# Narrow products in a position table, a second bank for two blocks' transposes, and VectorE rows for the last routed tile

## The chip, the cores and the metric

The program runs on one core of one Trainium2 chip. The metric is the device time of one execution in microseconds (us). The kernel before was timed three times: 1193.30, 1194.58 and 1198.49 us; the median, 1194.58 us, is its time.

## The reference, cut to what matters

One layer of a decoder trunk on 1024 tokens of width 1024, in fp32: a mixing half (attention beside a convolution), a residual sum, a second RMS norm, and a mixture of 32 experts (top 1 of 4 groups, then the top 2 of that group's 8 experts), another residual sum and a last norm. The change lies where the mixing half ends and the experts begin:

```
x = x + gt1 * mix
h2 = rms_norm(x, g_norm2[l]) * (1.0 + sc2) + sh2          # rows the experts read
# hier_moe, per token:
grp = argmax(h2 @ w_rg + b_rg)                              # 1 of 4 groups
top_val, top_idx = top_k(expert logits of that group, 2)    # 2 of its 8 experts
top_w = softmax(top_val) * p_grp
# per expert, on its tokens only:
y = (silu(xb @ w_gate[e]) * (xb @ w_up[e])) @ w_down[e]
x = x + gt2 * (sum over the token's two experts of top_w * y)
out = rms_norm(x, g_final)
```

## The kernel before, in words

**The stages.** The first half of the time is the mixing half. Then, tile by tile (`tt` 0 to 7, 128 tokens each), the output projection adds the residual (`second_norm`), makes the normed rows `h2`, stores them to DRAM (`h2d`), and routes the tile (`route`). The expert stage follows: expert after expert, a gather of the expert's rows from `h2d`, transposes, the gate and up products, a transpose of the hidden rows, the down products, and a scatter-add.

**Routing a tile.** `second_norm` sums the squares on ScalarE, forms the reciprocal root `r` on GpSimd (`rstd_of`, L93 and L94), transposes the raw rows to `xT` and returns `logits`, which multiplies by the router weights (L804) and scales by `r` (L806). The rows `h2 = x*r*a2b + sh2b` are made by two VectorE instructions (L794, L795) for tiles 0 to 6; for tile 7 GpSimd multiplies, ScalarE scales by `r` and GpSimd adds (L790 to L792). `route` is a chain of small VectorE instructions (L715 to L754), two products for the rank of each token in its expert, and two products (L760) that scatter token numbers and weights into the table `ptab` (4 values, 2 rounds of slots, 32 experts), summed over all tiles in one bank. After tile 7 the columns of the first four experts (`LO` = 4) are copied out (L881) and turned into the gather indices `early_t` (`tables`), the whole table is copied to `tb` (L883), and the first gathers may start.

**Position tables.** Experts from number 4 on are reordered at run time by how many tokens they have, so that some can be packed in half tiles (`PK`). `position_tables` does this in small steps between the products of the first two experts: it transposes the table (L1148), counts, ranks, and brings the columns into the new order with four groups of small products, the first two for packed experts in halves of 64 columns (L1202), the last two whole with 128 columns (L1205). From `pos`, which comes out of it, the queue of loads takes the number of every expert from 4 on.

**The expert stage.** Weights come through a ring of 8 buffers of 2 MB, filled by the sync queue (L595) in the order of use; a buffer is loaded again when its last reader is done. An expert that isn't packed has its weights split into a high and a low part, in four pieces per matrix, ScalarE making the high part (`ehi`, L102) and VectorE the low one (`elo`, L105); each product is done three times (high by high, high by low, low by high; L1028 to L1030). In this stage TensorE, VectorE and ScalarE run in the order in which the code is written. The rows of an expert are transposed in two steps of four 128x128 blocks (`x_steps`, L997), each into the tile `pt` of the pool `psx`, which has one buffer; ScalarE and VectorE then make `xh` and `xl` out of it. The pool `psg` has two buffers each for `pg` and `pu`, the sums of gate and up.

Ahead of the expert stage a scheduler orders the instructions of each engine.

Of the kernel before, what the change touches and what calls it, by code (L numbers as in the profile page):

```python
# [43 lines left out]
def trunk_kernel(ctx, tc, x, c, w_mod, b_mod, g_norm1, w_in, conv_w, conv_b, conv_ln_g, conv_ln_b,  # L44
# [663 lines left out]

    def route(tt, lg):
# [43 lines left out]
        for q in range(2):  # L753
            v.scalar_tensor_tensor(s0[:, :, :, q], rk[:, ks, None].to_broadcast([P, 2, 4]), float(P), Sf[:, ks, :],  # L754
                                   op0=OP.is_ge if q else OP.is_lt, op1=OP.mult)
        RH = wk3.tile([P, 2, 8, E], F32R, name="RH", bufs=1)
        v.tensor_tensor(RH, OH[:, ks, None, :].to_broadcast([P, 2, 8, E]),
                        s0.rearrange("p k a q -> p k (a q)")[:, :, :, None].to_broadcast([P, 2, 8, E]), op=OP.mult)
        for k in range(2):
            nc.tensor.matmul(ptab, onehots(8 * k + tt), RH[:, k, :, :], start=(tt == 0 and k == 0),  # L760
                             stop=(tt == 7 and k == 1), skip_group_check=True)
# [10 lines left out]
    def second_norm(tt, po):  # L772
# [8 lines left out]
        r = rstd_of(wk3, ss, 1, 1.0 / D)  # L781
        xT = mhp.tile([P, 8, P], F32, name="xT", tag=f"qk{2 + tt % 2}")
# [5 lines left out]
        if tt == 7:  # L788

            gp(h2, xt, a2b, OP.mult)  # L790
            nc.scalar.mul(h2, h2, r)
            gp(h2, h2, sh2b, OP.add)  # L792
        else:
            v.scalar_tensor_tensor(h2, xt, r, a2b, op0=OP.mult, op1=OP.mult)  # L794
            v.tensor_add(h2, h2, sh2b)  # L795
# [40 lines left out]
    for tt in range(2, 8):  # L836
# [3 lines left out]
        if tt % 4 == 3:  # L840
# [13 lines left out]

    early_t, late_t = [[rtc.tile([P, n], dt, name=f"{nm}{n}") for nm, dt in (("ti", I32), ("ws", F32))]
                       for n in (LO, E - LO + 1 + NOV)]

    half_t = [rtc.tile([P, E - LO + 1], dt, name=f"{nm}h") for nm, dt in (("ti", I32), ("ws", F32))]
    tb = rtc.tile([P, 4, 2, E], F32, name="tb")

    def slots(e):

        if e < LO:
            return [t[:, e:e + 1] for t in early_t]
        return [t[:, e - LO:e - LO + 1] for t in (half_t if e in PK else late_t)]

    def tables(tb, dst, pool, halves=False):

        ti, ws = dst
        n = tb.shape[-1]  # L870
        em = pool.tile([P, n], F32, name=f"em{n}", bufs=1)
        v.tensor_scalar(em, tb[:, 0, :], 0.0, BIG, op0=OP.is_equal, op1=OP.mult)
        if halves:
            v.scalar_tensor_tensor(em, tb[:, 0, :], -1.0, em, op0=OP.add, op1=OP.add)
            v.tensor_scalar(ti, em, 2.0, upper, op0=OP.mult, op1=OP.add)
        else:
            v.scalar_tensor_tensor(ti, tb[:, 0, :], -1.0, em, op0=OP.add, op1=OP.add)
        v.tensor_add(ws, tb[:, 2, :], tb[:, 3, :])

    t0 = wk3.tile([P, 4, LO], F32, name="t0", bufs=1)  # L880
    v.tensor_copy(t0, ptab[:, :, 0, 0:LO])  # L881
    tables(t0, early_t, wk3)
# [89 lines left out]
    def x_steps(e):  # L972
# [21 lines left out]
        def step(kk):  # L994
            pt = psx.tile([P, 4, P], F32, name="pt")
            for k in range(4):
                nc.tensor.transpose(pt[:, k, :], xt[:, 4 * kk + k:D:8], ident)  # L997
            split(xh[:, 4 * kk:4 * kk + 4, :], xl[:, 4 * kk:4 * kk + 4, :], pt)
# [138 lines left out]
    def position_tables():  # L1137
# [59 lines left out]
        for q, c0, c1, halves in jobs:  # L1197
            w = c1 - c0
            for a in range(4):
                sl = slice(o + a * w, o + a * w + w)  # L1200
                for h in range(2) if halves else ():
                    nc.tensor.matmul(c[64 * h:64 * h + 64, sl], tT[:, q, a, 0:64], pi[:, c0:c1], start=True, stop=True,  # L1202
                                     skip_group_check=True)
                if not halves:
                    nc.tensor.matmul(c[:, sl], tT[:, q, a, :], pi[:, c0:c1], start=True, stop=True, skip_group_check=True)  # L1205
# [233 lines left out]
```

## Time and profile before

| what | value |
|---|---|
| times | 1193.30, 1194.58, 1198.49 us |
| the profiled execution's own time | 1195.03 us |
| its span, first to last instruction | 1193.2 us |
| TensorE busy | 1079.5 us (90%) |
| VectorE busy | 784.2 us (66%) |
| ScalarE busy | 514.3 us (43%) |
| GpSimd busy | 232.0 us (19%) |
| DMA, mean over the span | 245 GB/s |
| mean granted TensorE clock | 0.957 of full speed |

The span is 1.8 us shorter than the execution's time; what lies around it is not touched here. In the rows below, PE is TensorE's products, PEld its weight loads, DVE is VectorE, ACT ScalarE, POOL GpSimd, and SPq the queue from which SyncE issues transfers. PEclk is the granted clock of TensorE: 1.00 is 2.4 GHz and 0.50 is 1.2 GHz. A product's busy time is longer than the distance to the next product, since products overlap; distances are read from the starts.

### The profile page before, as it was taken

The page shows a single profiled execution, that of the slowest core. Times are in us where ns is not written, and L with a number is a line of the kernel's source. Part 1 is how long each engine was busy: PE and PEld are TensorE (multiplying, and loading weights), DVE is VectorE, ACT ScalarE, POOL GpSimd, SP SyncE. Part 2 cuts the span into 40 slices and gives each one's busy share as a digit, 9 for nine tenths or more (in the row PEclk, how much of TensorE's full clock was granted, in tenths as well). Part 3 has the DMA queues.
Part 4 walks back from the last instruction along what each step waited for, and adds up shares of the span by engine and source line. Part 5 has one row for each costly group of instructions (what it writes and reads, how often), then busy time and mean ns, then how long its engine had stood idle before and what let it go on. Part 6 is the DMA issues. An engine that isn't in the chain of part 4 may idle for free. (4 is left out here: it accounts for less than half of the span.)

```text
span 1193.2 us, 16040 instructions
## 1 busy us (share of the span) xinstructions
PE 1079.5 (90%) x5876; PEld 788.5 (66%) x5876; DVE 784.2 (66%) x1300; ACT 514.3 (43%) x801; POOL 232.0 (19%) x204
## 2 busy tenths in 40 slices
PE   3899999999899999999789999999979998898960
PEld 0667777777566666888667877777656676576740
DVE  1457999992765656767658866666654586485833
ACT  2431112112767664322346655555553474364613
POOL 2340000003312104100211322222211131231112
PEclk9799999999799999999879999999999999999995
DMA  9542624302011005834757999999999999999947
GB/s 365 203 150 81 247 106 165 117 1 88 1 36 36 1 1 204 319 142 177 299 196 258 352 396 408 407 401 378 394 390 383 391 383 374 381 399 373 392 127 288
DMA packets 60829, 292.65 MB, mean 245 GB/s; under 512 B 11862, under 2 KB 16214, under 8 KB 33093
## 3 DMA queue, kind: packets, MB, share of 16 engines
q1 hardware_dynamic: 48020, 253.16, 54.2%
q0 software_dynamic: 11296, 34.17, 10.0%
q10 hardware_dynamic: 1424, 4.20, 0.9%
q8 instruction: 48, 0.79, 0.3%
q14 instruction: 41, 0.33, 0.1%
HBM read 275.75 MB, written 26.23 MB: 253 GB/s over the span
## 5 line engine op out<-in xcount | busy, mean ns | idle before, releaser
L105 DVE TENSOR_TENSOR elo<-raw,ehi 128x1024 fp32r<-128x1024 f32 x228 | 270.6, 1219 | 95.0 <-ACT ehi L102 93.4
L102 ACT CAST ehi<-raw 128x1024 fp32r<-128x1024 f32 x228 | 234.1, 1049 | 101.5 <-DMA raw<-in_w_exp_down_dram 36.7
L317 DVE SCALAR_TENSOR_TENSOR cv<-cv,cwT 128x1024 f32<-128x1024 f32 x120 | 154.1, 1284 | 3.6
L269 PE MATMUL pb<-hT,whi 128*128 128x512 f32 x256 | 100.8, 394 | 1.7 <-POOL hT L98 1.3
L268 PE MATMUL pb<-hT,whi 128*128 128x512 f32 x256 | 101.7, 399 | 0.0
L270 PE MATMUL pb<-hT,wlo 128*128 128x512 f32 x256 | 100.3, 392 | 0.6 <-DVE wlo L105 0.6
L1104 PE MATMUL py<-ehi,hh 128*128 128x512 f32 x152 | 63.4, 417 | 8.2 <-ACT ehi L102 6.7
L1073 POOL DMA_INDIRECT x1d<-ys,ti x19 | 44.9, 2361 | 129.2 <-DVE ys L1117 114.3
L1105 PE MATMUL py<-elo,hh 128*128 128x512 f32 x152 | 61.7, 406 | 4.4 <-DVE elo L105 4.4
L1028 PE MATMUL pg<-ehi,xh 128*128 128x512 f32 x152 | 62.5, 412 | 0.0
L268 PEld LDWEIGHTS pb<-hT,whi 128*128 128x128 f32 x256 | 48.1, 188 | 21.8 <-ACT whi L102 9.2
L1106 PE MATMUL py<-ehi,hl 128*128 128x512 f32 x152 | 60.6, 399 | 0.9 <-DVE hl L105 0.9
L1029 PE MATMUL pu<-elo,xh 128*128 128x512 f32 x152 | 60.1, 395 | 0.7 <-DVE elo L105 0.7
L1029 PE MATMUL pg<-elo,xh 128*128 128x512 f32 x152 | 60.5, 398 | 0.0
L1030 PE MATMUL pg<-ehi,xl 128*128 128x512 f32 x152 | 60.5, 398 | 0.0
L1028 PE MATMUL pu<-ehi,xh 128*128 128x512 f32 x152 | 59.9, 394 | 0.0
L1030 PE MATMUL pu<-ehi,xl 128*128 128x512 f32 x152 | 59.8, 393 | 0.0
L269 PEld LDWEIGHTS pb<-hT,whi 128*128 128x128 f32 x256 | 48.1, 188 | 13.0 <-POOL hT L98 2.9
L916 POOL DMA_INDIRECT xe<-h2d,ti x20 | 28.6, 1430 | 138.8 <-PE pt L997 122.9
L1017 PE MATMUL pu<-raw,x 128*64 128x256 f32 x448 | 51.6, 381 | 4.2 <-DMA raw<-in_w_exp_up_dram 4.2
L270 PEld LDWEIGHTS pb<-hT,wlo 128*128 128x128 f32 x256 | 48.1, 188 | 10.7 <-DVE wlo L105 1.0
L422 ACT ACTIVATE ns<-ns,st 128x128 f32<-128x128 f32 (+7 forms) x64 | 49.2, 772 | 9.2 <-DVE st L418 8.6
(276 smaller groups left out, 2203.5 us busy)
## 6 DMA issues: line engine op xcount, KB each, us to landing
raw<-in_w_exp_gate_dram SPq DMA_DIRECT2D x64, 1024.0 KB
raw<-in_w_exp_up_dram SPq DMA_DIRECT2D x64, 1024.0 KB
raw<-in_w_exp_down_dram SPq DMA_DIRECT2D x64, 1024.0 KB
wm<-in_w_mod_dram POOLq DMA_DIRECT2D x16, 1024.0 KB, 5.1
wm<-in_w_mod_dram SPq DMA_DIRECT2D x8, 1024.0 KB
raw<-in_w_in_dram SPq DMA_DIRECT2D x3, 2048.0 KB
xt<-in_x_dram SPq DMA_DIRECT2D x8, 512.0 KB
raw<-in_w_in_dram SPq DMA_DIRECT2D x4, 1024.0 KB
```

Of the source, the lines that this page charges most:

```text
L102: nc.scalar.copy(hi, src)
L105: nc.vector.tensor_sub(lo, src, hi.bitcast(F32))
L268: nc.tensor.matmul(p[half], hi[:, k, :], hT[0][:, k, sl], start=(k == 0), stop=False)
L269: nc.tensor.matmul(p[half], hi[:, k, :], hT[1][:, k, sl], start=False, stop=False)
L270: nc.tensor.matmul(p[half], lo[:, k, :], hT[0][:, k, sl], start=False, stop=(k == 7))
L317: nc.vector.scalar_tensor_tensor(y, u[:, j:j + T], w, y, op0=OP.mult, op1=OP.add)
L1028: nc.tensor.matmul(o, xh[:, k, :], hi[:, kk, :], start=(k == 0), stop=False)
L1029: nc.tensor.matmul(o, xh[:, k, :], lo[:, kk, :], start=False, stop=False)
L1030: nc.tensor.matmul(o, xl[:, k, :], hi[:, kk, :], start=False, stop=(k == 7))
L1104: nc.tensor.matmul(o, hh[:, k, :], hi[:, half, :], start=(k == 0), stop=False)
L1105: nc.tensor.matmul(o, hh[:, k, :], lo[:, half, :], start=False, stop=False)
L1106: nc.tensor.matmul(o, hl[:, k, :], hi[:, half, :], start=False, stop=(k == 3))
```

## The change

Three places are edited.

- `position_tables`: the last two groups of products (to the tables of the experts that aren't packed) are done as the first two are, in halves of 64 columns of weights, the upper half of the result in partitions 64 to 127.
- `x_steps`: for the first two experts the second step of four transposes goes to a buffer of `pu` in the pool `psg`, not to `pt` again.
- Tile 7: `h2` is made on VectorE, the multiplication by `a2b` right behind the sum of squares, the scaling by `r` and the sum in one instruction. In `route`, the columns of the first four experts have a small right side of their own (`RE`), products of their own (L789), and are copied and turned into `early_t` ahead of the rest of the table, which comes in four products (L799, L801) where there were two.

```diff
+        oh = [onehots(8 * k + tt) for k in range(2)] if tt == 7 else []
+        if tt == 7:
+            RE = wk3.tile([P, 2, 4, LO], F32R, name="RE", bufs=1)
+            v.tensor_tensor(RE, OH[:, ks, None, 0:LO].to_broadcast([P, 2, 4, LO]),
+                            s0[:, :, :, 0, None].to_broadcast([P, 2, 4, LO]), op=OP.mult)
+            for k in range(2):
+                nc.tensor.matmul(ptab[:, :, 0, 0:LO], oh[k], RE[:, k, :, :], start=False, stop=(k == 1),
+                                 skip_group_check=True)
+            t0 = wk3.tile([P, 4, LO], F32, name="t0", bufs=1)
+            v.tensor_copy(t0, ptab[:, :, 0, 0:LO])
+            tables(t0, early_t, wk3)
         RH = ...
         for k in range(2):
-            nc.tensor.matmul(ptab, onehots(8 * k + tt), RH[:, k, :, :], ...)
+            if tt == 7:
+                nc.tensor.matmul(ptab[:, :, 0, LO:], oh[k], RH[:, k, 0:8:2, LO:], ...)
+                nc.tensor.matmul(ptab[:, :, 1, :], oh[k], RH[:, k, 1:8:2, :], ...)
+            else:
+                nc.tensor.matmul(ptab, onehots(8 * k + tt), RH[:, k, :, :], ...)
...
         r = rstd_of(wk3, ss, 1, 1.0 / D)
+        if tt == 7:
+            v.tensor_mul(h2, xt, a2b)
...
         if tt == 7:
-            gp(h2, xt, a2b, OP.mult)
-            nc.scalar.mul(h2, h2, r)
-            gp(h2, h2, sh2b, OP.add)
+            v.scalar_tensor_tensor(h2, h2, r, sh2b, op0=OP.mult, op1=OP.add)
...
-    t0 = wk3.tile([P, 4, LO], F32, name="t0", bufs=1)
-    v.tensor_copy(t0, ptab[:, :, 0, 0:LO])
-    tables(t0, early_t, wk3)
     v.tensor_copy(tb, ptab)
...
         def step(kk):
-            pt = psx.tile([P, 4, P], F32, name="pt")
+            if kk and e < 2:
+                pt = psg.tile([P, F], F32, name="pu").rearrange("p (k t) -> p k t", k=4)
+            else:
+                pt = psx.tile([P, 4, P], F32, name="pt")
...
             for a in range(4):
                 sl = slice(o + a * w, o + a * w + w)
-                for h in range(2) if halves else ():
-                    nc.tensor.matmul(c[64 * h:64 * h + 64, sl], tT[:, q, a, 0:64], pi[:, c0:c1], ...)
-                if not halves:
-                    nc.tensor.matmul(c[:, sl], tT[:, q, a, :], pi[:, c0:c1], ...)
+                for h in range(2):
+                    s0 = 0 if halves else 64 * h
+                    nc.tensor.matmul(c[64 * h:64 * h + 64, sl], tT[:, q, a, s0:s0 + 64], pi[:, c0:c1], ...)
```

The definitions of `early_t`, `late_t`, `half_t`, `tb`, `slots` and `tables` also move up, ahead of `route`, unchanged.

Where the scheduler put the new instructions is seen in the order of the built programs. The first place is VectorE in tile 7, where its logits come in. `ohr` are the one-hot rows of tile 6, `lg` are the logits, `h_` is the tile `h2`, `xr` the raw rows, and `ng` the first result of the routing chain. Before:

```order
L706 TENSOR_SCALAR ohr<-cs,sv 128x128 [waits DVE_49]
L706 TENSOR_SCALAR ohr<-cs,sv 128x128
L806 SCALAR_TENSOR_TENSOR lg<-pt,rstd,crow 128x36 [waits PE_49,Pool_49]
L715 ISA ng,sm<-lg,zer 128x4 [waits DVE_49]
L715 ISA sm 128x1
```

Of the change, at the same place:

```order
L706 TENSOR_SCALAR ohr<-cs,sv 128x128 [waits DVE_49]
L706 TENSOR_SCALAR ohr<-cs,sv 128x128
L827 TENSOR_TENSOR h_4748<-xr,a2b 128x1024 [waits DMAHW5_49,Activation_49]
L850 SCALAR_TENSOR_TENSOR lg<-pt,rstd,crow 128x36 [waits PE_49,Pool_49]
L836 SCALAR_TENSOR_TENSOR h_4748<-h_4748,rstd,sh2b 128x1024 [waits DVE_49]
L741 ISA ng,sm<-lg,zer 128x4 [waits DVE_49]
L741 ISA sm 128x1
```

The two wide instructions stand on either side of the logits; the second of them stands between the logits and the routing chain.

The second place is VectorE at the end of tile 7's routing, where the indices `ti` of the first gathers are made (`t_` is `t0`, `elo` the first low part of the expert stage). Before:

```order
L757 TENSOR_TENSOR RH<-OH,s_4817 128x512 [waits DVE_49]
L706 TENSOR_SCALAR ohr<-cs,sv 128x128 [waits DVE_49]
L706 TENSOR_SCALAR ohr<-cs,sv 128x128
L881 COPY t_4836<-ptab 128x16 [waits PE_49]
L883 COPY tb<-ptab 128x256
L872 TENSOR_SCALAR em_4838<-t_4836 128x4 [waits DVE_49]
L878 TENSOR_TENSOR ws_4830<-t_4836 128x4
L877 SCALAR_TENSOR_TENSOR ti_4829<-t_4836,em_4838 128x4 [waits DVE_49]
L105 TENSOR_TENSOR elo<-raw,ehi 128x1024 [waits DMAHW5_49,DMAHW7_49,DMAHW1_49,Activation_49]
```

Of the change:

```order
L786 TENSOR_TENSOR RE<-OH,s_4823 128x32 [waits DVE_49]
L795 TENSOR_TENSOR RH<-OH,s_4823 128x512 [waits DVE_49]
L706 TENSOR_SCALAR ohr<-cs,sv 128x128 [waits DVE_49]
L706 TENSOR_SCALAR ohr<-cs,sv 128x128
L792 COPY t_4834<-ptab 128x16 [waits PE_49]
L727 TENSOR_SCALAR em_4836<-t_4834 128x4 [waits DVE_49]
L733 TENSOR_TENSOR ws_3603<-t_4834 128x4
L732 SCALAR_TENSOR_TENSOR ti_3602<-t_4834,em_4836 128x4 [waits DVE_49]
L898 COPY tb<-ptab 128x256 [waits PE_49]
L105 TENSOR_TENSOR elo<-raw,ehi 128x1024 [waits DMAHW7_49,DMAHW1_49,Activation_49]
```

`RE` is one instruction more; the wide `RH` still stands ahead of the one-hot rows and of the copy, while the copy of the whole table has moved behind the indices.

The third place is TensorE at the first expert's transposes (`xe_` are its gathered rows). Before:

```order
L1148 MATMUL py<-ident,tb 32x128 x7
L997 MATMUL pt<-ident,xe_4864 128x128 [waits DMASW4_49]
L997 MATMUL pt<-ident,xe_4864 128x128 x3
L997 MATMUL pt<-ident,xe_4864 128x128 [waits DVE_49]
L997 MATMUL pt<-ident,xe_4864 128x128 x3
L1028 MATMUL pg<-ehi,xh 128x512 [waits Activation_49]
```

Of the change:

```order
L1166 MATMUL py<-ident,tb 32x128 x7
L1015 MATMUL pt<-ident,xe_4869 128x128 [waits DMASW4_49]
L1015 MATMUL pt<-ident,xe_4869 128x128 x3
L1015 MATMUL pu<-ident,xe_4869 128x128 [waits PE_49]
L1015 MATMUL pu<-ident,xe_4869 128x128 x3
L1046 MATMUL pg<-ehi,xh 128x512 [waits Activation_49]
L1047 MATMUL pg<-elo,xh 128x512 [waits DVE_49]
L1048 MATMUL pg<-ehi,xl 128x512 [waits DVE_49]
```

The second four transposes wait for TensorE's own earlier work in place of VectorE; the wait for VectorE's `xl` has moved to the third product.

## Rows read from the trace of the kernel before

**Rows 1.** Stretches of the expert stage: bounds, length, busy time of each engine, clock, DMA

```profile
602.00:626.00 24.00, 21.28 (x111) 17.56 (x112) 11.54 (x24) 10.69 (x14) 0.99 (x1) 0.72 0.61 209
...
660.00:700.00 40.00, 40.00 (x224) 32.10 (x223) 33.33 (x36) 26.03 (x31) 9.73 (x5) 1.00 0.98 368
...
750.00:800.00 50.00, 50.00 (x274) 37.41 (x272) 36.08 (x39) 27.91 (x34) 10.77 (x7) 1.00 1.02 406
```

**Rows 2.** Waits of the load queue, 660 to 750: waiter, releaser: us, times, longest

```profile
SPq L595 <- DVE elo L105: 37.2, 16, 3.0
```

**Rows 3.** Waits of the load queue, 750 to 850

```profile
SPq L595 <- DMA raw<-in_w_exp_gate_dram: 28.2, 12, 3.8
```

**Rows 4.** Timeline, tile 7 to the first gather: start, us, instruction, idle before it

```profile
584.02 1.65 PE L804 MATMUL pt<-wr,xT 128*128 128x36 f32 x14
...
585.77 0.55 POOL L94 TENSOR_TENSOR rstd<-rstd,mhalf 128x1 f32<-128x1 f32 x1
...
586.35 0.25 DVE L806 SCALAR_TENSOR_TENSOR lg<-pt,rstd,crow 128x36 f32<-128x36 f32 x1 [2.76 <-POOL rstd L94]
...
587.57 2.34 POOL L98 TENSOR_TENSOR h<-h,sh2b 128x1024 f32<-128x1024 f32 x1 [0.36 <-ACT h L791]
...
587.74 2.22 DVE L721 CUSTOM_DVE_ANT_1 el<-lg,pen 128x32 f32<-128x32 f32 x1
...
593.50 0.69 DVE L757 TENSOR_TENSOR RH<-OH,s 128x512 fp32r<-128x512 f32 x1
...
594.44 0.80 PE L760 MATMUL ptab<-RH,ohr 128*128 128x256 f32 x2 [1.11 <-DVE ohr L706]
595.27 0.18 DVE L881 COPY t<-ptab 128x16 f32<-128x16 f32 x1 [0.69 <-PE ptab L760]
...
595.89 0.16 DVE L877 SCALAR_TENSOR_TENSOR ti<-t,em 128x4 int32<-128x4 f32 x1
...
596.35 2.01 POOL L916 DMA_INDIRECT xe<-h2d,ti  x1 [6.44 <-DMA gt2b<-modd]
```

**Rows 5.** Single lines over all tiles: ns min/median/max, first and last start

```profile
L721 DVE CUSTOM_DVE_ANT_1 el<-lg,pen x8: 181/192/2216, 501.1 to 587.7; 128x32 f32<-128x32 f32 x8
...
L794 DVE SCALAR_TENSOR_TENSOR h<-xr,rstd,a2b x7: 1281/1285/1285, 490.0 to 569.4; 128x1024 f32<-128x1024 f32 x7
...
L795 DVE TENSOR_TENSOR h<-h,sh2b x7: 1215/1224/1226, 491.8 to 570.7; 128x1024 f32<-128x1024 f32 x7
```

**Rows 6.** Timeline, the first expert's transposes

```profile
601.95 0.92 PE L997 MATMUL pt<-ident,xe 128*128 128x128 f32 x4 [2.71 <-DMA xe<-h2d,ti]
...
603.57 0.69 DVE L105 TENSOR_TENSOR xl<-pt,xh 128x512 fp32r<-128x512 f32 x1 [2.87 <-ACT xh L102]
...
604.32 1.12 PE L997 MATMUL pt<-ident,xe 128*128 128x128 f32 x4 [1.45 <-DVE xl L105]
...
605.09 0.78 PE L1028 MATMUL pg<-ehi,xh 128*128 128x512 f32 x1
```

**Rows 7.** Timeline, the reordering products (two records each)

```profile
618.32 1.09 PE L1202 MATMUL py<-ys 32*64 32x28 f32 x32
...
619.34 3.56 PE L1205 MATMUL py<-ys 32*128 32x28 f32 x16
```

**Rows 8.** Timeline, the second expert's transposes

```profile
628.02 0.68 DVE L105 TENSOR_TENSOR xl<-pt,xh 128x512 fp32r<-128x512 f32 x1
...
628.76 0.71 PE L997 MATMUL pt<-ident,xe 128*128 128x128 f32 x4 [2.29 <-DVE xl L105]
...
630.37 0.63 PE L1029 MATMUL pg<-elo,xh 128*128 128x512 f32 x1
...
630.80 0.63 PE L1030 MATMUL pg<-ehi,xl 128*128 128x512 f32 x1
```

**Rows 9.** Stretches around the second expert's start, columns as in rows 1

```profile
619.40:626.10 6.70, 6.70 (x27) 6.02 (x26) 1.31 (x2) 0.72 (x3) 0.00 (x0) 0.50 0.54 186
...
629.80:632.95 3.15, 3.15 (x10) 2.47 (x9) 0.69 (x1) 0.50 (x2) 0.94 (x1) 0.50 0.86 323
633.00:642.00 9.00, 9.00 (x41) 7.46 (x40) 8.00 (x20) 7.78 (x9) 0.00 (x0) 1.00 0.39 132
```

More of the change, by code (lines that the diff above doesn't have):

```diff
@@ L707, in onehots, with slots, tables @@
         return o
+    early_t, late_t = [[rtc.tile([P, n], dt, name=f"{nm}{n}") for nm, dt in (("ti", I32), ("ws", F32))]
+                       for n in (LO, E - LO + 1 + NOV)]
+    half_t = [rtc.tile([P, E - LO + 1], dt, name=f"{nm}h") for nm, dt in (("ti", I32), ("ws", F32))]
+    tb = rtc.tile([P, 4, 2, E], F32, name="tb")
+    def slots(e):
+        if e < LO:
+            return [t[:, e:e + 1] for t in early_t]
+        return [t[:, e - LO:e - LO + 1] for t in (half_t if e in PK else late_t)]
+    def tables(tb, dst, pool, halves=False):
+        ti, ws = dst
+        n = tb.shape[-1]
+        em = pool.tile([P, n], F32, name=f"em{n}", bufs=1)
+        v.tensor_scalar(em, tb[:, 0, :], 0.0, BIG, op0=OP.is_equal, op1=OP.mult)
+        if halves:
+            v.scalar_tensor_tensor(em, tb[:, 0, :], -1.0, em, op0=OP.add, op1=OP.add)
+            v.tensor_scalar(ti, em, 2.0, upper, op0=OP.mult, op1=OP.add)
+        else:
+            v.scalar_tensor_tensor(ti, tb[:, 0, :], -1.0, em, op0=OP.add, op1=OP.add)
+        v.tensor_add(ws, tb[:, 2, :], tb[:, 3, :])
     def route(tt, lg):
@@ L759, in route @@
         for k in range(2):
-            nc.tensor.matmul(ptab, onehots(8 * k + tt), RH[:, k, :, :], start=(tt == 0 and k == 0),
-                             stop=(tt == 7 and k == 1), skip_group_check=True)
+            if tt == 7:
+                nc.tensor.matmul(ptab[:, :, 0, LO:], oh[k], RH[:, k, 0:8:2, LO:], start=False, stop=(k == 1),
+                                 skip_group_check=True)
+                nc.tensor.matmul(ptab[:, :, 1, :], oh[k], RH[:, k, 1:8:2, :], start=False, stop=(k == 1),
+                                 skip_group_check=True)
+            else:
+                nc.tensor.matmul(ptab, onehots(8 * k + tt), RH[:, k, :, :], start=(tt == 0 and k == 0), stop=False,
+                                 skip_group_check=True)
     def products(po, parts, ks):
@@ L852, in trunk_kernel @@
     wop0.release()
[L855 to L878, printed above, removed]
-    t0 = wk3.tile([P, 4, LO], F32, name="t0", bufs=1)
-    v.tensor_copy(t0, ptab[:, :, 0, 0:LO])
-    tables(t0, early_t, wk3)
     v.tensor_copy(tb, ptab)
@@ L994, in step @@
         def step(kk):
[L995 removed]
+            if kk and e < 2:
+                pt = psg.tile([P, F], F32, name="pu").rearrange("p (k t) -> p k t", k=4)
+            else:
+                pt = psx.tile([P, 4, P], F32, name="pt")
             for k in range(4):
@@ L1200, in position_tables @@
                 sl = slice(o + a * w, o + a * w + w)
-                for h in range(2) if halves else ():
-                    nc.tensor.matmul(c[64 * h:64 * h + 64, sl], tT[:, q, a, 0:64], pi[:, c0:c1], start=True, stop=True,
-                                     skip_group_check=True)
-                if not halves:
-                    nc.tensor.matmul(c[:, sl], tT[:, q, a, :], pi[:, c0:c1], start=True, stop=True, skip_group_check=True)
+                for h in range(2):
+                    s0 = 0 if halves else 64 * h
+                    nc.tensor.matmul(c[64 * h:64 * h + 64, sl], tT[:, q, a, s0:s0 + 64], pi[:, c0:c1], start=True,
+                                     stop=True, skip_group_check=True)
             cols.append((o, w))
```

## The prediction, made before the result was known

> **What bounds the kernel now.** I read the stretches of the expert stage first. From 660 us on TensorE is busy the whole time, and the DMA share goes from 0.98 to 1.02; between 602 and 626 TensorE has 21.28 of 24.00 us, at a mean clock of 0.72, and the DMA share is only 0.61 [rows 1]. The waits of the load queue say which of the two sets the pace: up to 750 a load waits for the last reader of its buffer, mostly VectorE's low part, so the loads follow the compute [rows 2]; from 750 on a load waits for other loads, so the transfers are full and set the end [rows 3]. The end is therefore the time at which the load stream fills up plus a fixed rest. Whatever lets the first two experts start and finish earlier moves every later buffer release, and so the whole stream, by as much. The stretch from tile 7's logits (585 us) to the second expert's products (633 us) holds idle transfers, so time taken out there should reach the end in full. I then read that stretch in order of time; all three edits lie in it.
>
> **Tile 7 (start of the expert stage).** VectorE waits 2.76 us for `r` before it scales the logits at 586.35, since GpSimd does its wide multiplication between the two steps of `r`; the logit products were done at 584.02 + 1.65 = 585.67 [rows 4]. Without GpSimd's multiplication `r` is there in time: the new wide product on VectorE takes 1.22 us (as L795, [rows 5]) in an idle gap of 2.76 us. So the logits are scaled at about 585.75, 0.6 us earlier. Behind them stands the second wide instruction, 1.28 us (as L794, [rows 5]), with the whole routing chain queued behind it on VectorE; less the pause of some 0.1 us that a dependent instruction leaves anyway, the chain begins 0.6 us later than now. What it gets in return is one instruction: the masked minimum L721 takes 2.22 us in tile 7 and 0.19 us in the median of eight tiles [rows 4, 5]; in tile 7 it ends within 0.1 us of GpSimd's wide addition, 587.57 + 2.34 = 589.91, against 587.74 + 2.22 = 589.96. I read that as VectorE held by GpSimd, and the addition is gone: 2.0 us less. Net -1.4 us. If the long minimum had another cause, this part is +0.6.
>
> At the end of the chain `RE` adds one small instruction, about 0.15 us (128 by 32 elements, the size of L721). The wide `RH` (0.69 us) is not moved off the path: it still stands ahead of the one-hot rows. The two products fall from 256 columns to 16; they took 0.80 us together [rows 4], of which the columns are less than half, so I take 0.3 us off. The index `ti` started 0.62 us after the copy, with the whole table's copy between; without it I take 0.2 us off. Together -0.35. The first gather, issued 0.3 us after the index was done (595.89 + 0.16), then moves by -1.4 - 0.35 = -1.75 us. The row names a transfer as its releaser, but the distance from the index is that of any such issue, so I take the index for the cause. The store of the `h2` rows, which the gather also needs, moves more: its rows were ready at 589.91 and will be at about 587.2. The rest of the table now takes four products and a later copy; its transposes follow, and they have room, since TensorE waits 2.71 us for the gathered rows [rows 6]. Bounds: +0.25 (minimum still long: +0.6 - 0.35) to -3.3 (the gather, ahead of the next load's traffic, lands up to 1.5 us faster). I take -1.8.
>
> **First expert's transposes.** The second four wait 1.45 us until VectorE has emptied the one bank; the first product comes at 605.09 [rows 6]. With a second bank they run at once. The first product then needs `xh`, ready when VectorE starts `xl` at 603.57, so it starts near 603.6: -1.5 us; `xl` at 604.26 is in time for the third product. I take the wait itself, -1.45. The price of `pu`: the up sum uses the other of its two buffers, and that is free. Bounds 0 (some other wait on that bank) and -1.5.
>
> **Second round of the position table.** The first round, 32 records with 64 columns of weights, takes 619.34 - 618.32 = 1.02 us, 32 ns each; the second, 16 records with 128 columns, takes 3.56 us, some 220 ns each [rows 7]. The clock differs: the second round ran at half rate [rows 9]. At worst that doubles the 32 ns. So 32 narrow records cost 1.0 us at full and 2.0 us at half rate, and the gain is between 1.5 and 2.5; I take -2.0. Bounds from the same rows: 32 records at 220 ns would be 7.0 us, +3.5; at the other end -2.5. I lie by the narrow row, since it has the same shape and engine half.
> The Trainium skill, page "TensorE: Matmul & The Clock Gate", section "LDWEIGHTS (loading the stationary operand)", says that a weight load is priced by its columns alone. By that rule 32 loads of 64 columns cost what 16 of 128 do, the term would be 0, and the sum would be 2.0 us smaller; the trace disagrees so far, since the clock explains a factor of 2 between the two rounds and they differ by 6.8 per record. It is a rival below.
>
> **Second expert's transposes.** The second four wait 2.29 us for VectorE's `xl`, which comes late because ScalarE and VectorE first do a weight piece; the third product, the first to need `xl`, starts at 630.80, though `xl` was done at 628.70 [rows 8]. Without the wait it can start at about 628.8: -2.0 us. Bounds 0 and -2.3.
>
> **The clock.** Products follow each other every 9.00/41 = 0.22 us at full rate [rows 9] and every 630.80 - 630.37 = 0.43 us at half [rows 8]. The rate was half from 619.4 to 626.1, where some 6 products stand behind the second round, and from 629.8 to 632.95, with 7 more [rows 9]; before the first fall TensorE did only the small products, before the second it waited for the transposes. These 13 products lost 13 x 0.21 = 2.7 us. The change shortens both thin stretches but removes neither, so I give back about a third: -0.8. Bounds +2.7 (as many again at half rate) and -2.7.
>
> **Sum.** -1.8 - 1.45 - 2.0 - 2.0 - 0.8 = -8.05 us against the profiled execution's 1195.03 us: 1187.0 us. That execution is 0.45 us over the median of 1194.58 us, well within the spread of the three runs.
>
> **The rivals.**
> *Weight columns are the price.* The narrow products gain nothing: 1195.03 - 6.05 = 1189.0 us. For it: the columns are the same in total. Against it: the 32 ns.
> *The minimum stays long.* Then the wide instruction on VectorE only costs: the first part is +0.25 in place of -1.8, 1189.0 us as well. For it: one case of eight proves little. Against it: the common end within 0.1 us.
> *The gain is swallowed by the transfers.* If the load stream is in truth full from 640 us on, and not fed by the compute, an earlier start fills it no earlier: about 1194 us. For it: a DMA share of 0.98 [rows 1]. Against it: the queue's waits [rows 2] and the 0.61 earlier.
> *More than that.* No fall of the clock behind the table (-2.7, not -0.8) and a gather ahead of the load traffic (-1.5 more): 1195.03 - 8.05 - 1.9 - 1.5 = 1183.6 us.
> *Slower.* One mechanism: TensorE, with eight transposes in a row, narrow products and no wide ones, is granted the half rate for longer. Its place is the first expert's products, some 48 at 0.22 or 0.43 us, 9 of them slow now. The other terms sum to -7.25, so it decides from 7.25/0.21 = 35 more slow products; with all 39 others slow the time is 1195.03 - 7.25 + 8.2 = 1196.0 us. For it: the rate fell twice in this stretch around thin work. Against it: it came back within the first expert now, with a longer gap.
> The Trainium skill, the same page, section "Part 4: PE-mode transpose", says that transposes don't count as activity for the clock, which speaks for this one; no row here shows transposes alone for long enough.
>
> **How the numbers follow.** The forecast has 0.50, with a range of its own of 1184.5 to 1189.5; the columns 0.12, the long minimum 0.08, the swallowed gain 0.11, more than that 0.14, slower 0.05. A measurement of this kernel tells about 0.5% from no change, 6.0 us, so faster means under 1188.6. Faster: three quarters of the forecast (0.375), all of more (0.14), four tenths of the two at 1189.0 (0.08): 0.59. Slower by that much, over 1200.5, needs the clock rival with the second expert slow as well, or something unseen: 0.04. Within: 0.37. The range leaves out the top of the swallowed gain, the slower case and the fastest corner: 1182.5 to 1193.0 us.
>
> **What would show it.** In the new profile: L747, the minimum, at 0.2 us in tile 7, and the first gather near 594.6; the two sets of transposes of each of the first two experts with no wait between; all 64 narrow records within 2 to 3 us; the first product of the second expert about 7 us earlier than 629.80; loads waiting for loads from about 742 on. A first gather later than 596.4, or narrow records at 100 ns and over, or an unchanged time of the last load with an earlier second expert, would make the prediction wrong, each at its own term.

## The result, and the profile after

The changed kernel takes 1182.22 us in the median of 4 runs (1180.75 to 1183.84), the kernel before 1195.41 us in 4 runs on the same chip: a ratio of 0.9892, interval 0.9868 to 0.9917. It is faster, by about 13 us here. Two later sets of six runs gave 1183.31 us (0.9923, 0.9894 to 0.9951) and 1184.51 us (0.9935, 0.9913 to 0.9956); over all runs the medians are 1183.46 us (16 runs) and 1193.89 us (65 runs), so the change is worth some 10 us. The forecast was 1187.0 us, a gain of 8.05, with a range that began at 1182.5: the direction was right and the waits went as foreseen, but the gain was too small by some 2 to 5 us, and 1182.22 lies below the range. The step that failed is the clock's term; the part on the prediction takes it up.

The profiled execution took 1183.84 us (span 1182.0). The timeline of the changed kernel, with columns as in [rows 4], from tile 7 to the second expert:

```profile
584.66 1.65 PE L848 MATMUL pt<-wr,xT 128*128 128x36 f32 x14
...
586.42 0.26 DVE L850 SCALAR_TENSOR_TENSOR lg<-pt,rstd,crow 128x36 f32<-128x36 f32 x1 [1.06 <-PE pt L848]
586.60 1.28 DVE L836 SCALAR_TENSOR_TENSOR h<-h,rstd,sh2b 128x1024 f32<-128x1024 f32 x1
...
588.72 0.19 DVE L747 CUSTOM_DVE_ANT_1 el<-lg,pen 128x32 f32<-128x32 f32 x1
...
593.39 0.60 PE L789 MATMUL ptab<-RE,ohr 128*128 128x16 f32 x2 [1.09 <-DVE ohr L706]
...
594.43 0.16 DVE L732 SCALAR_TENSOR_TENSOR ti<-t,em 128x4 int32<-128x4 f32 x1
...
594.89 1.19 POOL L931 DMA_INDIRECT xe<-h2d,ti  x1 [7.51 <-DVE ti L732]
...
595.88 3.62 PE L1166 MATMUL py<-ident,tb 128*32 128x128 f32 x16 [0.52 <-DVE tb L898]
...
599.53 0.77 PE L1015 MATMUL pt<-ident,xe 128*128 128x128 f32 x4
600.14 0.60 PE L1015 MATMUL pu<-ident,xe 128*128 128x128 f32 x4
601.10 0.69 DVE L105 TENSOR_TENSOR xl<-pt,xh 128x512 fp32r<-128x512 f32 x1 [0.74 <-ACT xh L102]
601.12 0.50 PE L1046 MATMUL pg<-ehi,xh 128*128 128x512 f32 x1 [0.38 <-ACT xh L102]
...
612.63 0.18 PE L1208 MATMUL py<-ones,caps 32*1 32x1 f32 x2 [1.28 <-DVE caps L1201]
612.74 3.01 PE L1221 MATMUL py<-ys 32*64 32x28 f32 x64
...
618.41 1.06 PE L1015 MATMUL pt<-ident,xe 128*128 128x128 f32 x4
619.26 1.06 PE L1015 MATMUL pu<-ident,xe 128*128 128x128 f32 x4
...
620.58 0.48 PE L1046 MATMUL pg<-ehi,xh 128*128 128x512 f32 x1
...
621.61 0.50 PE L1048 MATMUL pg<-ehi,xl 128*128 128x512 f32 x1 [0.32 <-DVE xl L105]
...
626.70 0.39 PE L1046 MATMUL pu<-ehi,xh 128*128 128x512 f32 x1
```

The last row is the second expert's first up product (`pu`; its gate products, `pg`, come first). In the kernel before these two products of the second expert were

```profile
629.80 0.78 PE L1028 MATMUL pg<-ehi,xh 128*128 128x512 f32 x1
...
636.85 0.39 PE L1028 MATMUL pu<-ehi,xh 128*128 128x512 f32 x1
```

Against [rows 4], the logits are scaled 0.11 us after their products end (586.42 against 584.66 + 1.65 = 586.31), where it was 0.68 us; the masked minimum L747 takes 0.19 us, not 2.22; the gather's issue itself takes 1.19 us, not 2.01. Against [rows 6] and [rows 8], the eight transposes of each of these two experts stand together, and the 1.45 and 2.29 us between them are gone. TensorE stood idle 2.71 us before the first transposes of the kernel before; now the table's transposes (L1166) reach to 595.88 + 3.62 = 599.50, and the expert's begin at 599.53.

The load queue shows how the lead travels. Some issues of the same weight loads, of the kernel before:

```profile
598.46 2.60 SPq L595 DMA_DIRECT2D raw<-in_w_exp_gate_dram  x2
...
637.95 2.85 SPq L595 DMA_DIRECT2D raw<-in_w_exp_gate_dram  x2
...
1125.73 2.83 SPq L595 DMA_DIRECT2D raw<-in_w_exp_down_dram  x2
```

and of the changed kernel:

```profile
598.12 2.60 SPq L595 DMA_DIRECT2D raw<-in_w_exp_gate_dram  x2
...
628.03 2.85 SPq L595 DMA_DIRECT2D raw<-in_w_exp_gate_dram  x2
...
1115.14 2.83 SPq L595 DMA_DIRECT2D raw<-in_w_exp_down_dram  x2
```

The lead is 0.34 us at the first of these pairs, 9.92 us at the second, between 9.90 and 9.94 us at every issue behind it up to 749 us, and 10.6 us at the last; the span is 11.2 us shorter. Nothing of it is given back. The waits of the changed kernel's load queue, 650 to 740 and 740 to 840 us, have the form of [rows 2] and [rows 3]:

```profile
SPq L595 <- DVE elo L105: 37.3, 16, 3.0
...
SPq L595 <- DMA raw<-in_w_exp_gate_dram: 28.5, 12, 3.8
```

Last, the stretches of the changed kernel, columns as in [rows 1]:

```profile
601.10:611.10 10.00, 9.98 (x42) 7.73 (x42) 7.47 (x19) 7.51 (x9) 0.90 (x1) 1.00 0.81 287
613.40:620.10 6.70, 6.70 (x62) 6.02 (x59) 2.50 (x4) 1.87 (x4) 0.00 (x0) 0.50 0.64 224
620.30:629.30 9.00, 8.68 (x41) 6.96 (x40) 7.11 (x18) 6.52 (x8) 1.22 (x1) 1.00 0.52 160
```

and one of the kernel before that stood in no row ahead of the prediction:

```profile
602.30:609.10 6.80, 5.35 (x18) 4.09 (x17) 1.38 (x2) 2.22 (x3) 0.99 (x1) 0.50 0.72 260
```

The number ahead of the DMA share is the granted clock, 0.50 being 1.2 of 2.4 GHz. The kernel before spends three stretches behind tile 7 at half rate: this one and the two of [rows 9], 6.8 + 6.8 + 3.4 = 17.1 us. The changed kernel has one, 6.8 us: the first expert's products ahead of the table now run at full rate, and so do the second expert's from the first on. The six up products of the first expert behind the table are still at half rate.

To compare kernels, every time below is counted from the start of tile 7's transposes of the same execution:

| kernel (profiled execution) | gather issued | first transposes | first product | first table product | second expert's first up product | half rate behind tile 7, us |
|---|---|---|---|---|---|---|
| before | 14.48 | 20.08 | 23.22 | 34.85 | 54.98 | 17.1 |
| after | 12.38 | 17.02 | 18.61 | 28.63 | 44.19 | 6.8 |
| only table | 14.47 | 20.24 | 23.24 | 34.98 | 52.86 | 17.1 |
| only banks | 14.48 | 19.86 | 21.29 | 32.25 | 47.12 | 6.8 |
| only route | 12.36 | 16.90 | 19.78 | 31.11 | 51.07 | 13.6 |
| after, second set | 12.37 | 16.91 | 18.60 | 28.62 | 41.95 | none |
| after, third set | 12.38 | 16.92 | 18.61 | 28.64 | 44.15 | 6.8 |
| fill first (on before) | 14.48 | 20.25 | 22.88 | 32.63 | 49.18 | 3.4 |
| fill all (on before) | 14.49 | 20.10 | 22.73 | 32.44 | 49.26 | 3.4 |
| GpSimd addition (on after) | 14.48 | 19.03 | 20.86 | 30.89 | 45.41 | 3.4 |
| fill table (on after) | 12.37 | 16.91 | 18.61 | 28.63 | 42.17 | none |
| fill route (on after) | 14.72 | 21.49 | 22.90 | 32.93 | 46.29 | 6.8, ended before the first product |

The last column leaves out another half-rate stretch, over tile 7's routing, which every one of these executions has (10.2 us; in GpSimd addition 13.7, in fill route 6.8).

The second expert's up products start 54.98 - 44.19 = 10.8 us earlier; its first product, of the gate, 47.94 - 38.07 = 9.9 us. The load queue's 9.92 us are counted from the start of the execution, in which tile 7 came 0.65 us later than before; counted from tile 7 they are 10.6, so the queue carries this gain to the end. What lies outside this stretch differs from execution to execution, whatever the kernel: tile 7's transposes start at 577.7 to 584.3 us in the thirteen profiles, and from the second expert's first up product to the end it is 554.4 to 557.3 us. So two profiled executions can differ by several microseconds for reasons that lie outside the edits.

The theory to test: each edit takes out its own wait, and beyond that the clock gives back several microseconds, because TensorE no longer stands idle ahead of its products. The rival: the clock gives little, and single terms were too small.

### The profile page after: what moved, and what is told of

The parts are those of the page before. It is cut to its first block, busy times and chain, and to the rows that moved or that the text cites. A ratio compares the mean times of both kernels' runs of the same rounds, so it can differ in the third digit from the quotient of the medians.

```text
span 1182.0 us, 16081 instructions
## 1 busy us (share of the span) xinstructions
PE 1081.5 (91%) x5896; PEld 790.6 (67%) x5896; DVE 784.1 (66%) x1303; ACT 513.0 (43%) x800; POOL 224.3 (19%) x202
## 5 line engine op out<-in xcount | busy, mean ns | idle before, releaser
L105 DVE TENSOR_TENSOR elo<-raw,ehi 128x1024 fp32r<-128x1024 f32 x228 | 271.0, 1221 | 91.9 <-ACT ehi L102 90.0
L422 ACT ACTIVATE ns<-ns,st 128x128 f32<-128x128 f32 (+7 forms) x64 | 49.2, 772 | 11.1 <-DVE st L418 10.5
```

What stands on the lines that cost most here:

```text
L105: nc.vector.tensor_sub(lo, src, hi.bitcast(F32))
```

## The experiments

**One part at a time.** Three kernels carry one edit each, and the changed kernel was timed beside them.

*Only the position table* is the kernel before with this edit:

```diff
-                for h in range(2) if halves else ():
...
+                for h in range(2):
+                    s0 = 0 if halves else 64 * h
...
```

> The kernel before with the second round of the position table in halves alone. Theory (the clock made the rest of the gain): the round goes from 3.56 us to 1.0 to 2.0 us, the first block's products stay at half rate as before, so the time falls by 1.6 to 2.6 us. Rival (the three edits simply add up to 13 us, and the table was worth more than I took): 4 us or more. Rival (price by weight columns): no change.

Measured: 1191.73 us (12 runs), 0.9985 (0.9964 to 1.0006), not told from no change. The 64 products, at half rate in part, in this kernel's timeline:

```profile
617.95 2.58 PE L1203 MATMUL py<-ys 32*64 32x28 f32 x64
```

It was 1.02 + 3.56 = 4.6 us in [rows 7], so the stage gains 2.0 us. That the edit is worth 2 us is compatible with the interval, and so is nothing.

*Only the banks* is the kernel before with

```diff
+            if kk and e < 2:
+                pt = psg.tile([P, F], F32, name="pu").rearrange("p (k t) -> p k t", k=4)
...
```

> The kernel before with the second bank for the transposes of the first two blocks alone. Theory: 1.45 + 2.0 us from the two waits, the first block's products still start at half rate because TensorE still idles 2.7 us for the gathered rows; in all 3.5 us less, up to 5 if the second block's clock no longer falls. Rival (additive terms): 6 us or more, with the first block at half rate.

Measured: 1187.38 us (6 runs), 0.994 (0.9916 to 0.9964): 6.5 to 7.2 us, depending on whether one takes the median of before in these runs (1193.89) or the ratio, where the prediction had 3.45 for both banks. The interval reaches from 4.3 to 10.0 us, so the expectation's 5 is not excluded. The stretches of its profile show where the clock comes in:

```profile
603.30:606.50 3.20, 3.20 (x10) 2.37 (x9) 1.38 (x2) 1.17 (x2) 0.98 (x1) 0.50 0.95 343
620.40:623.60 3.20, 3.20 (x14) 2.80 (x13) 1.48 (x2) 1.70 (x3) 0.00 (x0) 0.50 0.40 166
```

Two of three stretches at half rate shrink from 6.8 to 3.4 us (the rows lie inside them), and the third is gone. The wide reordering products run at full rate here:

```profile
616.54 1.09 PE L1205 MATMUL py<-ys 32*64 32x28 f32 x32
617.56 1.94 PE L1208 MATMUL py<-ys 32*128 32x28 f32 x16
```

At one rate, 16 wide records take 1.94 us (121 ns each), 32 narrow ones 617.56 - 616.54 = 1.02 us (32 ns): the narrow form still halves the time, so the columns are not the whole price, but its worth is 0.9 us at full rate and not 2.0. In this trace the narrow loads start in pairs, 7 ns apart, and take 133 ns each; the wide ones start 112 ns apart and take 187 ns. The Trainium skill, page "TensorE: Matmul & The Clock Gate", section "LDWEIGHTS (loading the stationary operand)", prices a weight load by its columns alone; by that the two rounds would cost the same, and they differ by 0.9 us.

*Only the route* is the changed kernel with both of these edits undone; the core of what remains:

```diff
-            gp(h2, xt, a2b, OP.mult)
-            nc.scalar.mul(h2, h2, r)
-            gp(h2, h2, sh2b, OP.add)
+            v.scalar_tensor_tensor(h2, h2, r, sh2b, op0=OP.mult, op1=OP.add)
```

> The kernel before with the routing of tile 7 alone. Theory: the masked minimum takes 0.2 us, the first gather is issued 2 us earlier and its rows land 3 us earlier, TensorE's idle time ahead of the first transposes shrinks from 2.7 to about 0.5 us; the one-bank wait stays, so it is open whether the clock holds: 3 us less if it falls in the first block, 5 if it does not. Rival (additive terms): 2 us less whatever the clock does.

Measured: 1187.68 us (12 runs), 0.9945 (0.9925 to 0.9964), about 6.6 us. In the table above the gather is issued 14.48 - 12.36 = 2.1 us earlier, the first product 3.4 us. The stretches at half rate:

```profile
604.60:608.00 3.40, 3.40 (x10) 2.65 (x9) 0.97 (x2) 1.44 (x2) 0.99 (x1) 0.50 0.82 325
618.50:625.00 6.50, 6.50 (x25) 5.59 (x24) 1.27 (x2) 1.04 (x3) 0.00 (x0) 0.50 0.50 171
628.60:631.90 3.30, 3.30 (x9) 2.60 (x8) 0.69 (x1) 0.94 (x2) 0.70 (x1) 0.50 0.84 322
```

The first is halved here too, though the wait between the transposes is still there: what shrank is the idle time ahead of them. This profiled execution took 1193.76 us, the longest of the twelve, so its half-rate stretches need not be typical.

*The changed kernel again*, unedited:

> The changed kernel again, beside the parts on one chip. Theory: 11 to 13 us less than before, with the first block at the full rate, and 2 to 5 us more than the three parts alone add up to. Rival (additive terms): the parts alone sum to the whole within 1 us.

Measured: 1183.31 us (6 runs), 0.9923 (0.9894 to 0.9951). The expectation's theory fell: the parts alone sum to 1.8 + 7.2 + 6.6 = 15.6 us by the ratios, more than the whole's 9.2 in this set and not less. By the medians it is 14.9 to 10.6, and in the table above 2.1 + 7.9 + 3.9 = 13.9 to 10.8 or 13.0. A reading that fits is that banks and route each remove part of the same half-rate stretches, and what one has removed the other can't; but the excess is about as large as the intervals of the four ratios taken together, so it isn't shown that the rival of plain adding up is wrong. In this profile the clock does not fall behind tile 7 at all:

```profile
602.40:612.40 10.00, 10.00 (x42) 7.73 (x42) 7.47 (x19) 7.50 (x9) 0.73 (x1) 1.00 0.81 291
614.00:618.40 4.40, 4.40 (x80) 4.04 (x78) 2.81 (x3) 1.38 (x4) 0.00 (x0) 1.00 0.87 309
618.50:630.00 11.50, 10.76 (x48) 8.55 (x48) 9.30 (x22) 8.27 (x11) 2.04 (x1) 1.00 0.55 191
```

So one program has the fall behind the table in one execution and not in another; the second expert's up products start at 41.95 in place of 44.19, and those 2.2 us are what that one fall costs there.

**The clock by itself.** If the clock is a cause, work that only keeps TensorE busy in its waits should shorten the kernel before. *Fill first* adds ten useless products ahead of the first transposes of the kernel before:

```diff
+        fill = psg.tile([P, F], F32, name="pu")
+        for i in range(10):
+            nc.tensor.matmul(fill[:, 0:P], ident, ident, start=True, stop=True, skip_group_check=True)
         for f in steps(0):
```

> The kernel before, with ten products of 128 columns of no use put in the 2.7 us in which TensorE waits for the first gathered rows. Theory (the idle time ahead of the first block costs a clock fall): the clock no longer falls at the first block, its products up to the position table take 10.0 us in place of 11.6, and the loads of expert 4 are issued about 1.9 us earlier against tile 7. Rival (the clock falls for another reason): no difference in that stretch.

Measured: 1191.76 us (12 runs), 0.9993 (0.9974 to 1.0012), no change that can be told: by its times this test does not bear the theory out. The interval, 3.1 us less to 1.4 us more, holds both nothing and the expectation's 1.9 us. The one profile shows the mechanism:

```profile
600.31 2.50 PE L1304 MATMUL pu<-ident 128*128 128x128 f32 x20
603.22 0.71 PE L997 MATMUL pt<-ident,xe 128*128 128x128 f32 x4 [0.42 <-DMA xe<-h2d,ti]
605.38 0.71 PE L997 MATMUL pt<-ident,xe 128*128 128x128 f32 x4 [1.45 <-DVE xl L105]
```

The transposes take 0.71 us and not 0.92 [rows 6], and the first expert's block takes 32.63 - 22.88 = 9.75 us, where it was 34.85 - 23.22 = 11.63: the first stretch at half rate is gone, with the gather at its old place. In this execution the stretch behind the table is halved and the third is gone too, where nothing was edited, and the second expert's up products start 5.8 us earlier. The times of the twelve runs rule out that this is the usual gain; the profiled execution (1188.33 us) is the second shortest of them.

*Fill all* puts fillers into every wait of the kernel before: these ten, six in the table, and these between the transposes:

```diff
         def step(kk):
+            if kk and e < 2:
+                fill = psg.tile([P, F], F32, name="pu")
+                for i in range((6, 10)[e]):
+                    nc.tensor.matmul(fill[:, 0:P], ident, ident, start=True, stop=True, skip_group_check=True)
```

> The kernel before with products of no use in its four waits of TensorE behind tile 7: ten before the first gathered rows, six between the first expert's two sets of transposes, six in the position table, ten between the second expert's two sets. Nothing of the change is in it. Theory (about half of the gain is the clock): 4 to 7 us less than before, with no or one half-rate stretch of 3.4 us in the first two experts, and the second expert's up products some 6 us earlier against tile 7. Rival (the gain is all in the removed waits and the narrow products): the time of before or up to 1 us more.

Measured: 1189.17 us (12 runs) against 1193.31, 0.9968 (0.9952 to 0.9985): 4.1 us for work that computes nothing, the interval from 1.8 to 5.7 us. Three of this kernel's stretches:

```profile
604.20:613.80 9.60, 9.60 (x44) 7.72 (x42) 6.87 (x17) 7.63 (x9) 0.99 (x1) 1.00 0.58 201
618.90:622.20 3.30, 3.30 (x12) 2.71 (x11) 0.69 (x1) 1.12 (x4) 0.00 (x0) 0.50 0.53 221
622.30:630.00 7.70, 7.70 (x49) 6.88 (x49) 4.65 (x6) 4.02 (x6) 0.99 (x1) 1.00 0.52 175
```

One stretch of 3.4 us is left of 17.1, and the second expert's up products start at 49.26 in place of 54.98. The rival falls, by times and by profile: the waits are all still there, and what the clock gives back by itself is 4.1 us.

*Fill table* puts six such products into the 1.28 us wait ahead of the reordering products of the changed kernel:

```diff
+        for i in range(6):
+            nc.tensor.matmul(pp[:, 640:640 + P], ident, ident, start=True, stop=True, skip_group_check=True)
         nc.tensor.matmul(pp[0:1, 512 + E:512 + E + 1], caps[:, 1:2], ones[0:E, 0:1], start=True, stop=True,
```

> The changed kernel with six products of no use in the wait of 1.3 us between the two small products of the position table. Theory: the granted clock falls less often behind the table, where six products and twelve transposes follow; the time is 0 to 2 us less than that of the changed kernel, and its spread is smaller. Rival (the falls come from the narrow products themselves): no difference, or 0.2 us more for what does not fit in the wait.

Measured: 1180.59 us (5 runs), 0.9894 (0.9862 to 0.9927). The same kernel again, with the changed kernel beside it on one chip:

> The changed kernel beside the next two on one chip. Both theories: 10 to 13 us less than before. Theory (the clock): its half-rate stretch behind tile 7 is 7 us or less where the kernel before has some 17 us.

> The changed kernel with six products of no use in the position table's wait, now beside the changed kernel itself. Theory (the clock): 1 to 3 us less than the changed kernel, no half-rate stretch behind the first block. Rival (the earlier figure was chance): the same time.

Measured: the changed kernel 1184.51 us, with fillers 1181.19 us (6 runs), 0.9907 (0.9885 to 0.9928). Against the kernel before on the same chip, that is 8.8 and 12.1 us. Over all runs the two medians are 1183.46 (16) and 1180.7 (11): 2.8 us for six useless products. The intervals of the two ratios overlap, so 2.8 us is an estimate and not shown clear of noise. The profiles point the same way, since in both of the filled kernel the clock stays up where the changed kernel fell in two of three. The times of the profiled executions don't: the third set's, with the fall, took 1181.17 us, and the two filled ones, without it, 1184.11 and 1182.21, because tile 7 started at 578.7 us in the first and at 582.9 and 583.8 in the others. Timeline, then stretches:

```profile
612.50 1.60 PE L1209 MATMUL py<-ident 128*128 128x128 f32 x12
...
614.14 2.03 PE L1223 MATMUL py<-ys 32*64 32x28 f32 x64
```

```profile
612.50:616.60 4.10, 4.10 (x82) 3.89 (x81) 3.53 (x5) 2.06 (x4) 0.00 (x0) 1.00 0.87 278
616.70:620.00 3.30, 3.21 (x19) 2.45 (x17) 1.81 (x2) 2.02 (x3) 1.07 (x1) 1.00 0.70 271
```

By its medians this is the shortest version; against the kernel before that is clear, against the changed kernel it isn't.

**The long minimum.** *GpSimd addition* is the changed kernel with a wide addition on GpSimd put back, its result unused:

```diff
             v.scalar_tensor_tensor(h2, h2, r, sh2b, op0=OP.mult, op1=OP.add)
+            junk = wk3.tile([P, D], F32, name="xr")
+            gp(junk, h2, sh2b, OP.add)
```

> The changed kernel with a wide addition of two SBUF tiles on GpSimd, of no use, beside tile 7's routing chain, as the kernel before had one there. Theory (GpSimd held VectorE's masked minimum): a two-input instruction of the chain is held until the addition ends, 1.5 to 2.3 us, the first gather is issued that much later, and the time rises by 1.5 to 4 us against the changed kernel, by more than the delay where the clock falls again in the first block. Rival (the long minimum had another cause): the chain and the gather stay as in the changed kernel.

Measured: 1185.42 us (9 runs), 0.9924 (0.9899 to 0.9949); next to the changed kernel's three sets that is 1 to 3 us more, less than such runs can tell apart. GpSimd and VectorE in its profile:

```profile
586.09 2.34 POOL L98 TENSOR_TENSOR xr<-h,sh2b 128x1024 f32<-128x1024 f32 x1 [0.57 <-DVE sm L741]
...
586.12 2.33 DVE L700 TENSOR_SCALAR t<-ng,sm 128x4 f32<-128x4 f32 x1
...
588.95 0.19 DVE L747 CUSTOM_DVE_ANT_1 el<-lg,pen 128x32 f32<-128x32 f32 x1
```

The minimum is short, but another instruction, 128 by 4 elements and 0.23 us elsewhere, starts 0.03 us behind the addition and ends with it (588.43 and 588.45). The gather is back at 14.48. The wide addition is the cause of the hold; in both kernels it strikes the first instruction that VectorE begins behind the addition's start. The profile tells a second thing. With the gather at its old place, 14.48, the first transposes come at 19.03, in the kernel before at 20.08, so an earlier place after tile 7 isn't needed for the faster landing. The issue takes 1.19 us here and 2.01 there, and the next weight load is issued 3.2 us after the gather and not 2.1; which of the two counts isn't shown.

**Fillers in the routing.** *Fill route* put thirteen products ahead of the rank products of tile 7 and six ahead of the first expert of the changed kernel, to keep the clock up from tile 7 on (the second place is left out below):

```diff
+            for i in range(13):
+                nc.tensor.matmul(pr[:, P:2 * P], ident, h2s[0][:, 0:P], start=True, stop=True, skip_group_check=True)
```

> The changed kernel with thirteen products of no use behind tile 7's rows and six behind the table's transposes, where TensorE has nothing to do. Theory: the rank and table products of tile 7 run at the full rate, which moves the first gather by 0.3 to 0.6 us, and the first block stays at the full rate: 0 to 1 us less than the changed kernel. Rival (work of no use gets in the way): the first gather is not earlier, or the transposes wait for the fillers, up to 1 us more.

Measured: 1183.75 us (7 runs), 0.9924 (0.9897 to 0.9951), as the changed kernel. It says nothing for or against the clock, since the fillers got in the way; its timeline:

```profile
583.20 5.76 PE L772 MATMUL pt<-h,ident 128*128 128x128 f32 x26 [1.71 <-DVE sm L743]
...
596.70 2.65 PE L1327 MATMUL pg<-ident 128*128 128x128 f32 x12
```

Begun at half rate, the fillers took 5.76 us and overran the wait; the gather came 14.72 - 12.38 = 2.3 us later. The six behind the table's transposes held the first expert's up as well: its rows were there at 19.2, its transposes began at 21.49. So fillers can pay only where they end before the awaited operand comes.

**What the time follows.** Over the 23 runs of the kernel before that stand beside the single edits, time and mean granted clock go together with a correlation of -0.80 and -0.49 us for each 0.001 of clock; over the 12 runs of only table it is -0.94 and -0.68 us. The mean clock was 0.955 for the kernel before, 0.958 to 0.960 for the changed one, 0.9626 with fillers in the table. This is an association over whole runs, and much of it lies ahead of the edits: tile 7's transposes came earliest, at 577.7 and 578.7 us, in the two profiled executions (fill route, and the changed kernel's third set) whose granted clock up to there was 0.98; in the latest two, at 584.3 and 583.8, it was 0.96. The fillers are the test.

## Why the prediction was right or wrong, point by point

The profiled pair gained 10.8 us by the second expert's first up product, the forecast 8.05.

- **What bounds.** Right. The lead is carried through the load stream undiminished, so the rival of the swallowed gain fell. The second expert's first product came at 620.58, 9.2 us earlier than 629.80, where about 7 was the sign named.
- **Tile 7.** Right in mechanism: the minimum went from 2.22 to 0.19 us, the index moved by the table's shorter way, and the gather is issued 2.1 us earlier where 1.8 was taken. The rival of the long minimum fell by the experiment. What I had only as a bound, and put at nothing in the sum, came true in part: from the gather's issue to the first transposes it was 20.08 - 14.48 = 5.60 us and is 17.02 - 12.38 = 4.64, another 0.96. The bound's reason, the place ahead of the next load's traffic, may be right: the load comes 598.12 - 594.89 = 3.2 us behind the gather where it was 2.1. The issue is 0.8 us shorter as well.
- **First transposes.** Right: from transposes to product 3.14 us before and 1.59 after, 1.55 for the 1.45 taken.
- **Position table.** Right in sign, and in the profiled pair near in size (both rounds 4.6 us before, 3.01 after, the latter at half rate in its greater part, 1.6 for the 2.0 taken). The columns' rival fell. But at one rate the narrow form is worth 0.9 us: 3.56 - 1.94 = 1.6 us of the old second round were the half rate, and that part belongs to the clock.
- **Second transposes.** The wait went as foreseen; from the first table product to the second expert's first up product it was 20.13 us and is 15.56, 4.6 us for the 2.0 + 2.0 + 0.8 taken for table, transposes and clock together.
- **The clock: the step that failed.** I counted "13 products" behind the table, said that the change "shortens both thin stretches but removes neither", and gave back 0.8 us. There were three stretches, and the first, in the first expert's products, I had named only as a risk in the slower rival ("9 of them slow now"). It went altogether: first product to first table product fell from 11.63 to 10.02 us, 1.6 us for which the sum had nothing. [rows 1] already held it: a mean clock of 0.72 over 24 us is 0.28 / 0.5 x 24 = 13.4 us at half rate, and the stretch that I counted there, from 619.4 to 626, is 6.6. What changed is idle time: the 2.71 us ahead of the first transposes and the 1.45 us between them are gone. With the first wait filled and nothing else edited, the same block of the kernel before takes 9.75 us; with the wait between the transposes alone gone (only banks) 10.96, with the one ahead of them alone gone (only route) 11.33. Of the two stretches that I did count, the third is gone in all three profiles of the changed kernel, and the one behind the table comes in some executions only, at 2.2 us in the pair of profiles that differs by it.
- **The sizes together.** 0.3 (gather) + 0.96 (its landing) + 0.1 (first transposes) + 1.6 (first stretch) - 0.2 (the rest) = 2.7 us, the miss of the profiled pair. The median of the first four runs, 1182.22, is 4.8 us under the forecast; the rest of that is not traced to a term, and over all 16 runs the median is 1183.46. An estimate of the clock's whole part, from single profiles: the kernel before, with its clock up, would start the second expert's up products near 48 (49.2 in both filled kernels, less what their last 3.4 us at half rate cost, at most half of them). So 7 us of its 54.98 were clock; the changed kernel loses 2.2 or none of it, and the clock gives 5 to 7 us of the 10.8 to 13.0. The times by themselves show less: 4.1 us in fill all, and nothing that can be told in fill first.
- **More than that.** It named 1183.6 us, the nearest number, but its mechanism came true in part only: no fall behind the table in one of three profiles of the changed kernel, and 0.96 of the 1.5 us at the landing. The first stretch isn't in it. That the number is so near is partly luck.
- **Slower.** Fell. In all three profiles of the changed kernel the stretch behind the first expert's eight transposes is at 1.00. In only banks, where the 2.5 us of idle time ahead of them stayed, the clock fell 0.6 us after the eight began.

What stays open: why the clock falls behind the table in one execution of a program and not in another, how much of the landing's 0.96 us is the issue and how much the traffic, and whether the gains of the single edits overlap.

## What to carry to other kernels

Where the granted clock falls at a handover between stages, price each wait of TensorE twice: its own length, and the products behind it that run at half rate. Two edits that remove the same fall need not add up. Read such a gain from several executions, since the fall can come in one and not in the next. If a wait can't be removed, products that compute nothing and end before the operand comes can be worth microseconds. A load stream fed by buffer releases carries an early lead to the end of the kernel, so look first for idle time at the place where it starts.

## What the runs showed of the hardware that was not expected

- A wide GpSimd addition with two tensors holds even a one-tensor VectorE instruction of 128 by 4 elements until it ends: 2.33 us for 0.23. The Trainium skill, page "SBUF — State Buffer", section "SBUF: two separate sides", describes the port that the two engines share as locked for the whole instruction; the common end at 588.4 agrees.
- The issue of the gather takes 2.01 us in each of the kernels with the old route (before, only table, only banks, both filled ones of before), where three of VectorE's subtractions L105 run beside it, and 1.19 us in each with the new one (after, only route, GpSimd addition, fill table, fill route), where the first comes 0.6 to 0.9 us after the issue begins. No run here moves the subtractions alone, so that they are the cause isn't shown.
- Products that do little but load weights follow the granted clock: the 16 wide reordering records take 1.94 us at full and 3.56 us at half rate.
